# A quarter tile moved from the dense to the gathered half of an expert layer, with new pacing of the background work

## The chip, the cores and the metric
One core of one Trainium2 chip runs the whole kernel. The time is device microseconds of one execution. A profiled execution lists the busy time of each engine: PE is TensorE (PEld its weight loads), DVE VectorE, ACT ScalarE, POOL GpSimd, SP SyncE, which only issues transfers.

## The reference
One decoder block over 1024 tokens of width 1024, in float32. First a token mixer (a pooling branch and a forgetting attention of 16 heads, gated), then a channel mixer with 128 x 128 single-neuron experts, then a norm:

```python
h2 = modulate(rmsnorm(x, norm2_g), sh2, sc2)
q  = einsum('bsd,dk->bsk', h2, w_query)           # 8 heads x 2 halves x 128
sc = einsum('bshpc,hpnc->bshpn', q, sub_keys)     # 128 scores per half
# top 16 of each half, their 256 sums, top 16 of those: idx (expert), gates = softmax
a  = gelu(einsum('cd,chkd->chk', h2, peer_u[idx])) * gates
x += gt2 * einsum('chk,chkd->cd', a, peer_v[idx])
out = rmsnorm(x, final_g)
```

Each token thus uses 128 of the 16,384 experts (8 heads x 16).

## The kernel before, in words
**Precision.** Each float32 product is made of three TensorE passes over a high and a low part (`mm3`, lines 278 to 281). `split` (231) makes the parts: ScalarE writes the high one, VectorE or GpSimd subtracts for the low one. `load_w` (242) loads 512 KB of raw weights and splits them on the chip.

**Phases.** `PHASES` gives three runs of `phase` (481) over 512, 256 and 256 tokens (called pass or phase 1, 2 and 3 in the text, p = 0, 1, 2 in the code). Each projects and attends, head pair by head pair, then multiplies with `w_out` and then with `w_query` (the loop of line 779, 16 chunks), each chunk followed by scores and the top 16 per half on VectorE (lines 799 to 803). In the first phase `load_s` (259) splits the weights and stores both parts to memory; the later phases load both parts (1 MB per chunk) and split nothing.

**Experts, two ways.** A token tile is 128 tokens. Tiles 1 to 5 (`DT0`, `DT1`; 640 tokens, `ND`) are done densely: all 16,384 experts are computed for them and multiplied with a gate table that is zero where an expert isn't chosen. Tiles 0, 6 and 7 are done by gathering: for each of a token's 128 experts one indirect transfer (`gather`, 898) brings a row of 1024 values per token, 512 KB for 128 tokens, and VectorE takes a dot product (line 915) or adds a scaled row (925): 256 gathers a tile. They are issued on GpSimd's queue and turn in `GBUFS` = 3 buffers, in the dense stage in `GMORE` = 2 more.

**Background.** Three kinds of generators run beside the main work. `choose` (808), one per tile, turns the two lists of 16 into the 16 chosen experts and their gates, nearly all on VectorE. `gates` (941), one per dense tile, builds its part of the gate table in 32 rounds (GpSimd line 971, VectorE 973, TensorE 983, ScalarE 984) and stores it to `Gd`. `experts` (905) does a gathered tile. They are parts of the list `bg["todo"]`, taken in order. `tick(us)` (62) is called by the main work with a nominal duration (24 n x 0.00043 for a projection over n tokens); it adds us x `bg["rate"]` to a credit, and generators are advanced while the credit is positive, each `yield` costing what it states. `RATES` gives the rate in phase 2, from phase 3 on, in the dense stage, and from `w_out` of phase 3. `drain` empties the list at once.

**Dense stage.** `dense_experts` (1000): 16 groups. In the `up` half of a group 8 weight chunks (`ut`) each meet 2 halves of the 640 columns, 24 matmuls of 320 columns a half; GELU on ScalarE, the gate multiply (1026) and the split of the result on VectorE. In the `down` half 8 chunks (`vt`) sum over the group into `acc` (1042). A group's gate table (`Gg`, 2.5 MB, one buffer) is loaded at its first `up` (1012). The results of a half go through six PSUM banks. After the last group `finish_dense` (1048) transposes and norms the five tiles; then `drain` issues whatever is left.

The order on each engine is that of the program's issue, subject to the tile framework's own scheduling; `keep_in_program_order` pins the gathers.

Of the kernel before, what the change touches and what calls it, by code (L numbers as in the profile page):

```python
# [7 lines left out]
F = mybir.dt.float32  # L8
R = mybir.dt.float32r
# [8 lines left out]
D = 1024  # L18
# [8 lines left out]
DT0, DT1 = 1, 6  # L27
ND = (DT1 - DT0) * 128
# [12 lines left out]
RATES = (0.75, 0.6, 0.68, 0.7)  # L41
# [5 lines left out]
def block_kernel(ctx: ExitStack, tc: tile.TileContext, I, out, dbg=None):  # L47
# [173 lines left out]
    def rstd(ss):  # L221
        nc.vector.tensor_add(ss[:, 2:3], ss[:, 0:1], ss[:, 1:2])  # L222
        nc.scalar.activation(ss[:, 3:4], ss[:, 2:3], AF.Sqrt, scale=1.0 / D, bias=epsc)
        nc.vector.reciprocal(ss[:, 3:4], ss[:, 3:4])  # L224
        return ss[:, 3:4]
# [166 lines left out]
    def head2(c):  # L392
# [17 lines left out]
        fhl = c.big.tile([48, n], R, name="fhl", tag="fhl", bufs=1)  # L410
# [70 lines left out]
    def phase(c, nxt):  # L481
# [230 lines left out]
        if p == 2:  # L712
            bg["todo"].insert(0, gates(W["gb"], DT1 - 1))
# [32 lines left out]
        dl = [i for i in range(NQ) if DT0 <= qb0 + i < DT1]  # L746
        gl = [i for i in range(NQ) if i not in dl]
        if dl:
            T = slice(dl[0] * 128, dl[-1] * 128 + 128)
            o = (qb0 + dl[0] - DT0) * 128  # L750
            mv(h2dT[0][:, :, o:o + len(dl) * 128], h2h[:, :, T])
            mv(h2dT[1][:, :, o:o + len(dl) * 128], h2l[:, :, T])
            per = D // n
            for b, v in enumerate(tiles):
                mv(x1dT[:, b * per:(b + 1) * per, o:o + len(dl) * 128], v[:, :, T])
# [22 lines left out]
        tx = [sel.tile([128, PH, 2, 16], U32, name="mxi", tag="mxi", bufs=4) for _ in range(NQ)]  # L778
        for ch in range(16):
# [24 lines left out]
        store_parts()  # L804
        big.release()
        return nc_, [choose(qb0 + i, tv[i], tx[i]) for i in range(NQ)]

    def choose(tt, mv_, mx_):
        yield 0.0
        dense = DT0 <= tt < DT1  # L810
# [11 lines left out]
        yield 3.0  # L822
        ts = sel.tile([128, PH, 16], F, name="ts", tag="ts", bufs=1)
        ti = sel.tile([128, PH, 16], U32, name="ti", tag="ti", bufs=1)
        for h in range(PH):
# [6 lines left out]
            if h % 2:  # L832
                yield 1.8
# [31 lines left out]
        gt = sel.tile([128, PH, 16], F, name="gate", tag="gated" if dense else f"gate{tt}", bufs=1)  # L865
# [7 lines left out]
        if not dense or (dbg and "idx" in dbg):  # L873
            ix = sel.tile([128, 128], I32, name=f"idx{tt}")
# [4 lines left out]
        if dense:  # L879
            tr = W["gb"].tile([128, 3, 128], F, name="pairT", tag="pairT", bufs=DT1 - DT0)  # L880
# [5 lines left out]
        if dbg and "idx" in dbg:  # L886
            nc.sync.dma_start(dbg["idx"][tt * 128:(tt + 1) * 128], ix)
            nc.sync.dma_start(dbg["gate"][tt * 128:(tt + 1) * 128], gate[tt])

    X = {"i": 0, "p": None}  # L890
# [13 lines left out]

    def experts(tt):
        yield 0.0
        row = g_row("row")
        nc.sync.dma_start(row, h2d[tt])
        h2 = X["ps"].tile([128, D], F, name="h2", tag="gx", bufs=1)
        nc.scalar.activation(h2, row, AF.Copy)  # L910
        dots = gp.tile([128, 128], F, name="dots", tag="dots", bufs=1)
        for k in range(128):
            yield GSTEP
            g = gather(I["peer_u"], idx[tt][:, k:k + 1])
            nc.vector.scalar_tensor_tensor(g, g, 1.0, h2, op0=OP.mult, op1=OP.mult, accum_out=dots[:, k:k + 1])  # L915
        nc.scalar.activation(dots, dots, AF.Gelu)
        nc.vector.tensor_mul(dots, dots, gate[tt])
        acc = X["ps"].tile([128, D], F, name="acc", tag="gx", bufs=1)
        for k in range(128):
            yield GSTEP  # L920
            g = gather(I["peer_v"], idx[tt][:, k:k + 1])
# [262 lines left out]
```

## Time and profile before

| | |
|---|---|
| runs shown, us | 3359.74, 3362.7, 3367.93 (median 3362.7) |
| profiled execution, us | 3367.48 (span 3365.7) |
| busy in the span | PE 3132.3, DVE 2427.5, ACT 1267.7, POOL 1754.1 |
| instructions | 56,878 |
| DMA | 1004.60 MB, mean 298 GB/s |
| first and last dense matmul, us from the start | 1493.9, 3317.6 |

Busy time is the time in which an engine had at least one instruction under way; matmuls overlap, so a matmul's own duration (some 310 ns) is longer than the step to the next. PEclk is the granted TensorE clock as a share of 2.4 GHz. DMA share is the mean busy share of the core's 16 DMA engines. In a row of a chain or a wait, what stands after `<-` released the instruction.

### The profile page before, as it was taken

What the parts mean: (1) busy time and instruction counts of PE and PEld (TensorE: products, weight loads), DVE (VectorE), ACT (ScalarE), POOL (GpSimd) and SP (SyncE); (2) the same over time, 40 slices, a digit from 0 to 9 for tenths busy, and PEclk for the clock granted to TensorE, in tenths of its full rate; (3) what the DMA queues carried; (4) which work ended last, traced back from release to release, by engine and by line L of the source; (5) the groups of instructions that cost most, each with busy time, mean ns of one, the idle gap of its engine ahead of it and who ended that gap; (6) DMA issues with size and microseconds to landing.
All of it is one profiled execution on the core that took longest, in us unless ns stands there. A gap on an engine that the chain in (4) does not pass through costs nothing. (4 is left out here: it accounts for less than half of the span.)

```text
span 3365.7 us, 56878 instructions
## 1 busy us (share of the span) xinstructions
PE 3132.3 (93%) x20912; PEld 2992.4 (89%) x20912; DVE 2427.5 (72%) x5520; ACT 1267.7 (38%) x2405; POOL 1754.1 (52%) x1328
## 2 busy tenths in 40 slices
PE   6999889888799899888999999999999999999995
PEld 4778778778788798888999999999999999999994
DVE  5764556997958876768766777677677767777677
ACT  5555542346545565522222322232223222322231
POOL 1233233013324132414777787678777767777774
PEclk9999999899999999999999999999999999999997
DMA  8987787777789788783899899899998999989997
GB/s 330 332 299 261 271 297 270 240 231 235 226 304 313 226 268 269 259 311 139 306 333 332 320 328 337 318 348 332 339 329 321 322 330 344 346 319 337 329 337 252
DMA packets 373078, 1004.60 MB, mean 298 GB/s; under 512 B 34128, under 2 KB 146368, under 8 KB 370624
## 3 DMA queue, kind: packets, MB, share of 16 engines
q1 hardware_dynamic: 262208, 598.26, 51.7%
q0 software_dynamic: 110592, 402.70, 32.7%
q8 instruction: 166, 2.72, 0.3%
q14 instruction: 112, 0.92, 0.1%
HBM read 851.25 MB, written 149.58 MB: 297 GB/s over the span
## 5 line engine op out<-in xcount | busy, mean ns | idle before, releaser
L233 POOL TENSOR_TENSOR wl<-wr,wh 128x1024 fp32r<-128x1024 f32 x320 | 776.1, 2426 | 647.7 <-ACT wh L232 604.4
L232 ACT ACTIVATE wh<-wr 128x1024 fp32r<-128x1024 f32 x325 | 344.2, 1059 | 927.5 <-PE oT L280 536.1
L279 PE MATMUL oT<-ah,wh 128*128 128x320 f32 x2048 | 632.3, 310 | 10.0 <-ACT ah L232 10.0
L279 PE MATMUL z<-h2x,wh 128*128 128x320 f32 x2048 | 633.8, 310 | 3.3 <-ACT wh L232 1.7
L281 PE MATMUL z<-h2x,wl 128*128 128x320 f32 x2048 | 633.5, 310 | 1.4 <-POOL wl L233 1.3
L280 PE MATMUL oT<-al,wh 128*128 128x320 f32 x2048 | 633.0, 310 | 1.2 <-DVE al L233 1.1
L280 PE MATMUL z<-h2x,wh 128*128 128x320 f32 x2048 | 633.3, 309 | 0.0
L281 PE MATMUL oT<-ah,wl 128*128 128x320 f32 x2048 | 632.7, 310 | 0.0
L925 DVE SCALAR_TENSOR_TENSOR acc<-g,dots,acc 128x1024 f32<-128x1024 f32 x381 | 489.2, 1284 | 124.9 <-DMA g<-peer_v,idx 122.3
L915 DVE SCALAR_TENSOR_TENSOR g<-g,h 128x1024 f32<-128x1024 f32 x384 | 460.9, 1214 | 94.2 <-DMA g<-peer_u,idx 92.4
L900 POOL DMA_INDIRECT g<-peer_v,idx x384 | 362.0, 943 | 126.1 <-issue 45.7
L900 POOL DMA_INDIRECT g<-peer_u,idx x384 | 361.7, 942 | 124.1 <-issue 57.1
L279 PEld LDWEIGHTS oT<-ah,wh 128*128 128x128 f32 x2048 | 384.9, 188 | 10.5 <-ACT ah L232 10.5
L279 PEld LDWEIGHTS z<-h2x,wh 128*128 128x128 f32 x2048 | 385.0, 188 | 4.2 <-ACT wh L232 2.2
L281 PEld LDWEIGHTS z<-h2x,wl 128*128 128x128 f32 x2048 | 384.8, 188 | 2.4 <-POOL wl L233 2.4
L280 PEld LDWEIGHTS oT<-al,wh 128*128 128x128 f32 x2048 | 385.1, 188 | 1.8 <-DVE al L233 1.8
L281 PEld LDWEIGHTS oT<-ah,wl 128*128 128x128 f32 x2048 | 385.1, 188 | 0.0
L280 PEld LDWEIGHTS z<-h2x,wh 128*128 128x128 f32 x2048 | 384.9, 188 | 0.0
L971 POOL TENSOR_TENSOR o<-hi,lo 128x512 f32<-128x512 f32 x160 | 206.6, 1293 | 322.2 <-PE G L983 283.0
L279 PE MATMUL z<-hTh,wh 128*128 128x256 f32 (+1 forms) x840 | 290.0, 350 | 18.2 <-ACT hTh L232 8.4
L281 PE MATMUL z<-hTh,wl 128*128 128x256 f32 (+1 forms) x840 | 286.3, 341 | 1.0 <-DMA wl<-w_inl 0.8
L280 PE MATMUL z<-hTl,wh 128*128 128x256 f32 (+1 forms) x840 | 285.9, 340 | 1.3 <-DVE hTl L233 1.3
(286 smaller groups left out, 5938.0 us busy)
## 6 DMA issues: line engine op xcount, KB each, us to landing
wr<-ut SPq DMA_DIRECT2D x128, 512.0 KB
wr<-vt SPq DMA_DIRECT2D x128, 512.0 KB
Gd<-Gb SPq DMA_DIRECT2D x40, 1024.0 KB
Gg<-Gd SPq DMA_DIRECT2D x16, 2560.0 KB
wh<-w_inh SPq DMA_DIRECT2D x60, 512.0 KB
wl<-w_inl SPq DMA_DIRECT2D x60, 512.0 KB
wm<-w_mod SPq DMA_DIRECT2D x48, 512.0 KB
wr<-w_in SPq DMA_DIRECT2D x45, 512.0 KB
```

What stands on the lines that cost most here:

```text
L232: nc.scalar.activation(hi, src, AF.Copy)
L233: eng_lo.tensor_tensor(lo, src, hi.bitcast(F), op=OP.subtract)
L279: nc.tensor.matmul(ps, ah, bh, start=start, stop=False)
L280: nc.tensor.matmul(ps, ah, bl, start=False, stop=False)
L281: nc.tensor.matmul(ps, al, bh, start=False, stop=stop)
L900: d = nc.gpsimd.indirect_dma_start(out=g, out_offset=None, in_=table, in_offset=bass.IndirectOffsetOnAxis(ap=col, axis=0))
L915: nc.vector.scalar_tensor_tensor(g, g, 1.0, h2, op0=OP.mult, op1=OP.mult, accum_out=dots[:, k:k + 1])
L925: nc.vector.scalar_tensor_tensor(acc, g, dots[:, k:k + 1], acc, op0=OP.mult, op1=OP.add)
L971: nc.gpsimd.tensor_tensor(o2, hi[:, X, :, None].to_broadcast([128, 4, 8, 16]), lo[:, X, None, :].to_broadcast([128, 4, 8, 16]), op=OP.mult)
```

## The change
1. The dense part covers tokens 32 to 639 (`DA`, `DB`, 608 columns, halves of 304) instead of tiles 1 to 5. Gathered are tiles 5, 6, 7 and the first `HK` = 32 tokens of tile 0. These 32 x 128 rows are laid out as 128 partitions x 32: four blocks of 32 experts, each with a copy of the 32 tokens; so 32 gathers for `u`, 32 for `v`, and the four partial sums are added at the end.
2. This quarter tile runs as background in phase 3; if it isn't finished then, it goes on in the dense stage. Outside the dense stage its rows use SBUF (`x_tile`) and the three buffers.
3. `w_query` is loaded raw and split in every phase; nothing of it is stored.
4. The costs that `choose` states are half as high again, `RATES` are new, and the rate is 0 in the `w_query` loop. `choose` of tile 5 moves to the dense stage; there each `choose` stands right before its own `experts`.
5. A group's gate table is loaded in four parts, at the second, fourth, sixth and eighth `down` of the group before. The dense stage has one more pair of weight buffers.

```diff
-RATES = (0.75, 0.6, 0.68, 0.7)
+RATES = (0.95, 1.0, 0.8, 1.0)
...
+        if name == "w_query":
+            return load_w(I[name][i])
...
-            bg["todo"].insert(0, gates(W["gb"], DT1 - 1))
             bg["rate"] = RATES[3]
...
+        rate, bg["rate"] = bg["rate"], 0.0
         for ch in range(16):
...
         store_parts()
+        bg["rate"] = rate
...
-        yield 3.0
+        yield 4.5
...
-                yield 1.8
+                yield 2.7
...
-                        yield 0.8
+                        yield 1.2
...
-                yield 1.1
+                yield 1.6
...
     def experts(tt):
         yield 0.0
+        n, K = (HK, HK) if tt == HT else (128, 128)
         row = g_row("row")
-        nc.sync.dma_start(row, h2d[tt])
+        ix, gt = idx[tt], gate[tt]
+        if tt == HT:
+            ix = sel.tile([128, HK], I32, name="ixh", tag="ixh", bufs=1)
+            gt = sel.tile([128, HK], F, name="gth", tag="gth", bufs=1)
+            for b in range(128 // HK):
+                to, c = slice(b * HK, b * HK + HK), slice(b * HK, b * HK + HK)
+                nc.sync.dma_start(ix[to], idx[tt][:HK, c])
+                nc.sync.dma_start(gt[to], gate[tt][:HK, c])
+                nc.sync.dma_start(row[to], h2d[tt][:HK])
+        else:
+            nc.sync.dma_start(row, h2d[tt])
...
-        for k in range(128):
+        for k in range(K):
             yield GSTEP
...
+        if tt == HT:
+            for b in range(1, 128 // HK):
+                nc.sync.dma_start(r1[:n], r0[b * n:b * n + n])
+                nc.vector.tensor_tensor(r0[:n], r0[:n], r1[:n], op=OP.add)
+                r1 = g_row("r1")
...
-        for q in range(32):
+        for q in range(DA // 4 if tt == HT else 0, 32):
...
-        W["x"], W["m"], W["i"] = dd, 1, 2
+        W["x"], W["m"], W["i"] = dd, 2, 3
...
+        def load_gates(gr, part):
+            if part == 0:
+                A["G"] = dd.tile([128, NC16, 8, 16], F, name="Gg", tag="Gg", bufs=1)
+            C = slice(part * NC16 // 4, (part + 1) * NC16 // 4)
+            nc.sync.dma_start(A["G"][:, C], Gd[gr][:, C].rearrange("p c (i t) -> p c i t", i=8))
...
             wh, wl = load_w(I["vt"][gr * 8 + c], nc.gpsimd)
+            if gr < 15 and c % 2:
+                load_gates(gr + 1, c // 2)
...
-    late = [experts(tt) for tt in range(DT0)]
-    bg["todo"] = ch[:DT0] + [f for i in range(DT0, 4) for f in (ch[i], gates(gb, i))]
+    early = [experts(HT)]
+    bg["todo"] = [f for i in range(4) for f in (ch[i], gates(gb, i))]
     bg["rate"] = RATES[0]
     c, ch = phase(c, next_head(2))
     W["xq"].release()
-    bg["todo"] += [f for i in range(4, DT1) for f in (ch[i - 4], gates(gb, i))][:-1]
+    bg["todo"] += [ch[0], gates(gb, 4)] + early
+    late = ch[1:]
     bg["rate"] = RATES[1]
     c, ch = phase(c, lambda: None)
+    early = [f for f in bg["todo"] if f in early]
+    bg["todo"] = [f for f in bg["todo"] if f not in early]
     drain()
...
-    bg["todo"] = ch + late + [experts(tt) for tt in range(DT1, 8)]
+    bg["todo"] = early + [f for i, tt in enumerate(range(DT1, 8)) for f in ((late + ch)[i], experts(tt))]
     bg["rate"] = RATES[2]
     dense_experts()
```

## Rows read from the trace of the kernel before

**Rows 1.** Busy time by stretch: from and to in us, length, busy us of each engine with its instructions, then the granted clock, the DMA share and GB/s. The stretches: phase 2 up to its query loop, that loop, phase 3 in two halves up to `w_out`, its query loop, the start of the dense stage, its steady part, all of it.

```profile
605.00:980.00 375.00, 316.48 (x2358) 302.59 (x2359) 313.06 (x969) 203.71 (x449) 94.94 (x84) 0.91 0.75 244
980.00:1055.00 75.00, 71.83 (x588) 70.38 (x587) 56.29 (x274) 26.07 (x48) 24.33 (x23) 0.98 0.92 318
1055.00:1230.00 175.00, 155.90 (x1187) 144.86 (x1187) 155.14 (x481) 101.00 (x223) 50.03 (x51) 0.96 0.80 252
1230.00:1403.00 173.00, 159.89 (x1274) 152.86 (x1273) 117.67 (x237) 103.46 (x209) 57.53 (x50) 0.97 0.82 262
1425.00:1491.00 66.00, 57.02 (x431) 54.76 (x431) 35.95 (x214) 16.98 (x35) 7.25 (x4) 0.92 0.97 344
1493.90:1600.00 106.10, 91.55 (x577) 88.62 (x578) 96.04 (x329) 32.61 (x53) 43.45 (x24) 0.92 0.43 155
1600.00:3300.00 1700.00, 1700.00 (x11593) 1700.00 (x11593) 1219.76 (x1860) 456.56 (x737) 1278.95 (x981) 1.00 0.91 330
1493.90:3318.00 1824.10, 1809.55 (x12291) 1806.61 (x12292) 1332.53 (x2207) 489.17 (x790) 1331.28 (x1012) 1.00 0.88 319
```

**Rows 2.** Matmuls in order of time: start in us, duration, then line and shape. First and last of 51 in a row at 320 columns in the dense stage, of 18 at 256 in a query loop, of 20 at 512 in the first query loop.

```profile
1639.72 0.31 PE L280 MATMUL z<-h2x,wh 128*128 128x320 f32 x1
...
1647.06 0.31 PE L279 MATMUL z<-h2x,wh 128*128 128x320 f32 x1
...
1485.03 0.28 PE L279 MATMUL z<-h2h,wr 128*128 128x256 f32 x1
...
1487.03 0.28 PE L281 MATMUL z<-h2h,wr 128*128 128x256 f32 x1
...
551.62 0.39 PE L280 MATMUL z<-h2l,wh 128*128 128x512 f32 x1
...
555.97 0.39 PE L281 MATMUL z<-h2h,wl 128*128 128x512 f32 x1
```

**Rows 3.** The end, in order of time: the last dense matmul, the last norm of a dense tile, the last gather on GpSimd, the last operation of the last gathered tile.

```profile
3317.59 0.31 PE L281 MATMUL oT<-ah,wl 128*128 128x320 f32 x1
...
3344.49 1.40 DVE L1060 SCALAR_TENSOR_TENSOR Gg<-z,ss,h2x 128x512 f32<-128x512 f32 x2
...
3349.55 0.94 POOL L900 DMA_INDIRECT g<-peer_v,idx  x1 [3.76 <-DVE acc L925]
...
3360.77 1.28 DVE L938 SCALAR_TENSOR_TENSOR r<-r,ss,r 128x1024 f32<-128x1024 f32 x1
```

**Rows 4.** Groups of instructions by line and shape, background work: count, then busy us, mean ns of one, idle time before. Eight `choose` and five `gates` in all; lines 827 to 831 are a head's five steps, two of which are shown.

```profile
L858 DVE SCALAR_TENSOR_TENSOR cand<-pk 128x128 f32<-128x128 f32 x256 | 82.1, 457 | 0.1
L862 DVE TENSOR_REDUCE pk<-cand 128x128 f32<-128x1024 f32 x32 | 38.7, 1209 | 0.2
L828 DVE FIND_INDEX8 ti<-ts,cand 128x8 uint32<-128x96 f32 x64 | 15.2, 248 | 0.0
L829 DVE MATCH_REPLACE8 tmp<-ts,cand 128x96 f32<-128x96 f32 x64 | 15.0, 237 | 0.1
L973 DVE TENSOR_TENSOR o<-iota,pairT 128x512 f32<-128x512 f32 x160 | 133.6, 839 | 33.1 <-PE G L983 32.2
L958 DVE TENSOR_TENSOR lo<-iota,dg 128x256 f32<-128x256 f32 x40 | 17.3, 438 | 0.0
L958 DVE TENSOR_TENSOR hi<-iota,dg 128x128 f32<-128x128 f32 x40 | 11.8, 304 | 7.4 <-POOL o L971 7.4
```

**Rows 5.** The same view: the weight splits, and VectorE's own work in the dense stage.

```profile
L233 POOL TENSOR_TENSOR wl<-wr,wh 128x1024 fp32r<-128x1024 f32 x320 | 776.1, 2426 | 647.7 <-ACT wh L232 604.4 <-DMA kdh<-ks 10.3 <-PE pt L628 8.8
L232 ACT ACTIVATE wh<-wr 128x1024 fp32r<-128x1024 f32 x325 | 344.2, 1059 | 927.5 <-PE oT L280 536.1 <-PE z L280 191.7 <-DMA wr<-vt 134.3
L1026 DVE TENSOR_TENSOR z<-z,Gg 128x320 f32<-128x320 f32 x256 | 126.6, 495 | 66.2 <-ACT z L1024 64.4
L233 DVE TENSOR_TENSOR al<-z,ah 128x320 fp32r<-128x320 f32 x256 | 124.0, 485 | 22.7 <-ACT ah L232 22.6
L1042 DVE TENSOR_TENSOR accT<-accT,oT 128x320 f32<-128x320 f32 x240 | 116.0, 484 | 182.2 <-PE oT L281 182.0
```

**Rows 6.** The gathers' DMA queue over the span (packets, MB, share of 16 engines), and two stretches of 10 us in the dense stage (columns as in rows 1).

```profile
q0 software_dynamic: 110592, 402.70, 32.7%
...
2820.00:2830.00 10.00, 10.00 (x70) 10.00 (x69) 4.40 (x11) 0.00 (x0) 6.17 (x5) 1.00 1.00 419
...
2400.00:2410.00 10.00, 10.00 (x70) 10.00 (x69) 6.60 (x13) 1.38 (x2) 7.98 (x8) 1.00 0.96 326
```

**Rows 7.** VectorE's work per gather, by line and shape as in rows 4, and the time of a gather from issue to landing.

```profile
L925 DVE SCALAR_TENSOR_TENSOR acc<-g,dots,acc 128x1024 f32<-128x1024 f32 x381 | 489.2, 1284 | 124.9 <-DMA g<-peer_v,idx 122.3
L915 DVE SCALAR_TENSOR_TENSOR g<-g,h 128x1024 f32<-128x1024 f32 x384 | 460.9, 1214 | 94.2 <-DMA g<-peer_u,idx 92.4 <-DVE accT L1042 0.3
...
L915 DVE DVE_READ_ACCUMULATOR g<-g,h 128x1 f32 x384 | 31.7, 83 | 0.0
...
DMA to landing us min/median/max: 4.2/6.0/14.9
```

**Rows 8.** VectorE's rounds of the gate table (line 973) in the two halves of phase 3, and the index search of `choose` (line 858, 32 for one) in the first: length, busy us and count.

```profile
1055.00:1230.00 175.00, 25.79 (x33) 0.96 0.80 252
1230.00:1403.00 173.00, 32.02 (x39) 0.97 0.82 262
...
1055.00:1230.00 175.00, 19.18 (x64) 0.96 0.80 252
```

More of the change, by code (lines that the diff above doesn't have):

```diff
@@ L745, in phase @@
         z0, = to_T(c, x1, rsb, sc2, sh2, h2h, h2l, [("w_query", 0)])
[L746 to L752, printed above, removed]
+        lo, hi = max(t0, DA), min(t0 + n, DB)
+        gl = [i for i in range(NQ) if not DA <= t0 + i * 128 <= DB - 128]
+        if lo < hi:
+            T = slice(lo - t0, hi - t0)
+            O = slice(lo - DA, hi - DA)
+            mv(h2dT[0][:, :, O], h2h[:, :, T])
+            mv(h2dT[1][:, :, O], h2l[:, :, T])
             per = D // n
             for b, v in enumerate(tiles):
-                mv(x1dT[:, b * per:(b + 1) * per, o:o + len(dl) * 128], v[:, :, T])
+                mv(x1dT[:, b * per:(b + 1) * per, O], v[:, :, T])
         if gl:
@@ L809, in choose @@
         yield 0.0
-        dense = DT0 <= tt < DT1
+        dense = tt < DT1
+        gathered = tt == HT or not dense
         buf = sel.tile([128, 1024], F, name="cand", tag="cand", bufs=1)
@@ L860, in choose @@
                     if x % 4 == 3:
-                        yield 0.8
+                        yield 1.2
                 nc.vector.tensor_reduce(to, oh.rearrange("p h k x -> p (h k) x"), axis=AX.X, op=OP.add)
-                yield 1.1
+                yield 1.6
             nc.vector.tensor_add(dst, dst, pf)
-        gt = sel.tile([128, PH, 16], F, name="gate", tag="gated" if dense else f"gate{tt}", bufs=1)
+        gt = sel.tile([128, PH, 16], F, name="gate", tag="gate" if gathered else "gated", bufs=3 if gathered else 1)
         nc.vector.tensor_tensor(gt, ts, ts[:, :, 0:1].to_broadcast([128, PH, 16]), op=OP.subtract)
@@ L872, in choose @@
         gf = gt.rearrange("p h k -> p (h k)")
-        if not dense or (dbg and "idx" in dbg):
-            ix = sel.tile([128, 128], I32, name=f"idx{tt}")
+        if gathered:
+            ix = sel.tile([128, 128], I32, name=f"idx{tt}", tag="idx", bufs=3)
             nc.vector.scalar_tensor_tensor(ix, w0, 128.0, w1, op0=OP.mult, op1=OP.add)
@@ L885, in choose @@
             pairT[tt] = tr
[L886 to L890, printed above, removed]
+    X = {"i": 0, "p": None, "ps": None}
     def g_row(name):
@@ L1054, in finish_dense @@
                 for c in range(4):
-                    nc.tensor.transpose(pt[:, c * 128:(c + 1) * 128],
-                                        acc[:, hf * 4 + c, i * 128:(i + 1) * 128], ident)
-                nc.scalar.activation(yt[:, H], pt, AF.Square, accum_out=ss[:, hf:hf + 1])
-            rs = rstd(ss)
+                    nc.tensor.transpose(pt[:n, c * 128:(c + 1) * 128], acc[:, hf * 4 + c, T], ident)
+                nc.scalar.activation(yt[:n, H], pt[:n], AF.Square, accum_out=ss[:n, hf:hf + 1])
+            rs = rstd(ss, n)
             for pt, H in zip(ps, hs):
-                nc.vector.scalar_tensor_tensor(yt[:, H], pt, rs, fg[:, H], op0=OP.mult, op1=OP.mult)
-            nc.sync.dma_start(out[(DT0 + i) * 128:(DT0 + i + 1) * 128, :], yt)
+                nc.vector.scalar_tensor_tensor(yt[:n, H], pt[:n], rs, fg[:n, H], op0=OP.mult, op1=OP.mult)
+            nc.sync.dma_start(out[DA + T.start:DA + T.stop, :], yt[:n])
+        for part in range(4):
+            load_gates(0, part)
         for gr in range(16):
@@ L1074, in dense_experts @@
                 down(gr, i)
-        for i in range(DT1 - DT0):
-            finish_dense(i, rows, fg[:, 0])
+        for i in range((ND + 127) // 128):
+            finish_dense(i, rows[:, i * D:i * D + D] if i < 4 else fg[:, 1], fg[:, 0])
         W["m"], X["p"] = 0, None
```

61 lines of the change are left out of this document (34 added, 27 removed).

## The prediction
> **What bounds the kernel now.** Read first the table of stretches [rows 1], by stage. In the dense stage (1493.9 to 3318, 54% of the span) TensorE is busy in all 1700 us between 1600 and 3300, at granted clock 1.00, while the DMA engines are 0.91 busy at 330 GB/s and VectorE is at 72%: the stage is TensorE's own time, with little left on the transfers. The list of matmuls in order of time gives the step from one to the next: 7.34 us over 50 steps at 320 columns = 146.8 ns, 2.00 us over 17 at 256 columns = 117.6 ns, 4.35 us over 19 at 512 = 229 ns [rows 2], so the step goes with the columns (0.456 ns each between 256 and 320) and weights loaded for every matmul don't set it. 12,288 x 0.1468 = 1804 us of the stage's 1824. In the second and third attention phases (605 to 1491) no engine is full: VectorE is at 83%, 75%, 89%, 68% and 54% of the five stretches, TensorE at 84 to 96%, DMA at 0.75 to 0.97. There the order of work and the loads decide together. Last, the chain of waits: the span ends 48 us after the last dense matmul, on gathers still to be issued [rows 3].
>
> **Dense stage, columns.** 640 columns become 608, halves of 320 become 304; the count of matmuls stays. One step falls by 16 x 0.456 = 7.3 ns to 139.5; 12,288 x 7.3 ns = 90 us off, 1714 us left. Ends: 6.9 ns (the slope between 320 and 512, 0.428 ns) gives 84, and 0 if something else sets the pace (below).
> The row for 320 columns is 146.8 ns. The Trainium skill, TensorE: Matmul & The Clock Gate, section Back-to-back issue gap, gives a warm step of N/2.4 + 2.5 ns, 135.8 ns here; the trace does not agree in height or slope, and by it the saving would be 6.7 ns x 12,288 = 82 us instead of 90.
>
> **Dense stage, start.** From 1493.9 to 1600 TensorE loses 14.5 us and runs at mean clock 0.92: two `choose` runs stand first, 0.92 of VectorE is spent and no gather moves (DMA 0.43) [rows 1]. One `choose` costs VectorE about 34 us: 32 x 0.46 + 4 x 1.21 for the index search, 8 heads x 1.45 for the top 16, the rest small [rows 4]. Afterwards one stands there, at 34.3 planner units over rate 0.8 instead of two of 24 over 0.68. One planner unit of the stage lasts 1.066 us (24 matmuls are counted as 3.137 and take 24 x 0.1393 = 3.343). So 34 us of VectorE in 46 us beside the stage's own 21% (per group of 768 matmuls 16 x 0.47 + 16 x 0.46 + 16 x 0.46 = 22 of 107 us, [rows 5] times 0.95): 95%, it fits. I take 18 of the 20 us beyond 1804 as saved. Ends 0 and 20.
>
> **Dense stage, gathers.** 768 gathers of 524 kB remain (tiles 5, 6, 7 for 0, 6, 7). Each is paced at 1.46 units: before 1.46/0.68 x 1.066 = 2.29 us, after 1.46/0.8 x 1.066 = 1.94 us. Demand while they run, before: 0.524 MB/2.29 us = 229 GB/s, weights 0.524 per 48 matmuls (7.05 us) 74, gate table 2.62 MB per 768 matmuls 23: 327, as measured (330). After: 270 + 78 + 23 = 371 GB/s. The measured rate at full share is 330/0.91 = 363 [rows 1]; q0's own figures give 402.7 MB/(0.327 x 3365.7) = 366 [rows 6]. 371 is above either. The gathers' stretches last 1125.7 units /0.8 x 1.066 = 1499 us at TensorE's pace; at 363 GB/s they last 1499 x 371/363 = 1532. With gather DMAs late, VectorE, in order, holds the gate multiply behind them, PSUM fills and TensorE waits. I add 35 us, rounded. Ends: 0 (windows of 10 us reached 419 GB/s), and 206 if the ceiling is the 326 GB/s of a window with share 0.96 [rows 6]; 363 is the mean over the whole stage, so I take it. VectorE then needs 768 x 1.29 + 370 + 102 = 1463 us [rows 5, 7], 84%; GpSimd 2.43 per 48 matmuls and 0.94 per gather, also 85%: neither binds first.
> Full share and 419 GB/s stand in the row of a 10 us window [rows 6]. The Trainium skill, DMA: Bandwidth & Descriptors, section Where 436 GB/s comes from, lets the memory side bind at about 358 GB/s per core; the trace does not agree for a core alone, and with 358 the loss would be 54 us instead of 35.
> The gate table in four parts, issued while the group before is in its `down` half, takes SyncE's wait for the last gate multiply away from ahead of the `ut` loads; TensorE shows no wait in 1600 to 3300, so it is worth 0, and the same holds for the fourth pair of weight buffers. SyncE may wait at part 0 for the last multiply, with `vt` loads queued behind; the weight buffers cover that wait.
>
> **End.** The plan: 3 x (34.3 + 375.2) = 1228.7 units of background against a credit of 256 x 24 x 608 x 0.00043 x 0.8 = 1285, so gathers end about 56/0.8 x 1.066 = 75 us before the last matmul. Before it was 1174 against 1150, and some 16 were left. What follows the last matmul is then five transposes-and-norms of about 2 us each, a first one of 5 us and 4 us of writing: 20 us for 48. 28 us off; ends 0 and 32.
>
> **Query weights.** Pass 2 (980 to 1055) and pass 3 (1425 to 1491) read 16 x 1.05 MB, and 5.2 MB of `h2x` in pass 3: 23 MB in 66 us at share 0.97. After, 0.52 MB each: 14.4 MB, 42 us at that rate. What is late next: TensorE, 57 us busy in pass 3; the splits (ACT 1.06, GpSimd 2.43 per chunk, 17 and 39 us for 16, [rows 5]) hide under it, on a GpSimd 7 of 66 us busy. Background is at rate 0 there. I take 56 us for each: 19 and 10 off; ends 0 and 25 together with 33. In pass 1 the 16.8 MB of stores go: 2 us at most.
>
> **Phases, background.** Units in the code: phase 2 has 209.6 ticks outside the query loop x 0.95 = 199 credited; its list is 256.8 (4 x 34.3 + 23.9 + 3 x 31.9), so 57.7 goes over. Phase 3 adds 34.3 + 31.9 + 94.9 = 218.8 in all, against 205.1 + 21.1 = 226 at rate 1.0: the quarter tile just fits. In phase 2 outside the query loop VectorE's background is 3.25 x 34 + 2.75 x 33 = 201 us against 3.9 x 34 + 2 x 33 = 199: the same, evener. I take 8 off. Ends -15 and +15.
> Phase 3 (1055 to 1403, 348 us): VectorE does 272.8 us, of it two `choose` and 72 gate rounds of 0.839 + (0.438 + 0.304)/4 = 1.02 us [rows 1, 4, 8], own work 131. After: 131 + 1.75 x 34 + 64 x 1.02 + 64 x 1.29 for the quarter tile's gathers = 339 us, 97% of the old stretch. And DMA: 33.5 MB for 64 gathers = 92 us of full share, less 2 MB of gates, where 0.81 of 348 us = 282 is already spent: 369. So it cannot stay at 348. At phase 2's VectorE share (313/375 = 0.835) 339 us need 406; at full share of the DMA, 369. I take 401: +53. Ends +21 (the DMA sum) and the 3-buffer limit of rival 2. The copies of the quarter tile's rows and sums wait on SyncE for VectorE with weights queued behind, a few us inside this sum.
>
> **Sum.** -90 - 18 + 35 - 28 - 29 - 2 - 8 + 53 = -87 on the profiled execution's 3367.5 us (span 3365.7), 3280; the median of the runs, 3362.7, is 4.8 lower: 3276.
>
> **Rivals.** (1) The transfers' ceiling binds in the dense stage, ends slower: at 340 GB/s the gather stretches take 1499 x 371/340 = 1636, 137 instead of 35: 3378; it decides against the change from a loss of 122 us, a ceiling of 343. For it: 10 us windows with share 0.96 at 326. Against: 363 as the mean, 419 as best. (2) In phase 3 only three gather buffers turn: landing 6.0 us (4.2 to 14.9) + 1.3 + 0.4 over three is 2.6 us each [rows 7], 165 us for 64; at 14.9 it is 354 us, 189 more: 3465. It cancels the gain from a landing of 10 us. Against: the median. (3) Neither binds (phase 3 absorbs the quarter tile, DMA carries 371): 3276 - 35 - 53 = 3188; for it the 419 GB/s window and TensorE's 9% of unused time in phase 3. (4) The quarter tile isn't done by phase 3: up to 1323.6 units against 1285 leaves 26 gathers at the end, 60 us, but phase 3 is 38 shorter: 3298.
>
> **Chances.** Forecast 0.51 (3235 to 3325), (1) 0.13, (2) 0.09, (3) 0.23, (4) 0.04. Slower: 0.09 of (1) and 0.05 of (2); same: 0.04 and 0.03; the rest faster. 0.3% is 10 us, about what such a measurement can tell from none. The range reaches to both sides, 3200 to 3380.
>
> **What would show it.** Right: steps of 139 ns at 304 columns, small TensorE waits on gathers in the dense stage with DMA share over 0.95, no gather after the last matmul, the third phase some 50 us longer, both later query loops near 56 us. Wrong: TensorE below 90% in the dense stage, or a third phase over 480 us.

## The result and the profile after

The changed kernel takes 3412.4 us (median of 4 runs, 3401.7 to 3420.4) against 3362.4 for the kernel before: ratio 1.0145 (95% interval 1.0109 to 1.018), slower by about 50 us, where 3276 was predicted. Its profiled execution took 3418.5 us with a span of 3416.8. The traces of b_comb and b_inter72, two of the experiments below, were taken in slow executions and are not read; the medians are of fast ones.

The parts of the page of the changed kernel on busy time and on the DMA queues, and the shares by engine of the chain that ended last:

```profile
PE 3060.0 (90%) x20856; PEld 2914.0 (85%) x20856; DVE 2566.5 (75%) x5616; ACT 1291.5 (38%) x2445; POOL 1888.6 (55%) x1415
...
q1 hardware_dynamic: 257328, 563.56, 48.2%
q0 software_dynamic: 119808, 436.26, 35.0%
...
PE 49%; DVE 8%; DMA 5%; issue 2%; POOL 1%; ACT 1%; SPq 0%; POOLq 0%; DVEq 0%; ACTq 0%
```

TensorE has 72 us less to do than before (3132.3 then), VectorE 139 us more. Then the windows, with the columns of [rows 1]: phase 2, its query loop, phase 3 in two halves, its query loop, the start of the dense stage, the rest of it, and what follows the last dense matmul.

```profile
605.00:980.00 375.00, 322.66 (x2457) 308.36 (x2457) 312.12 (x873) 212.99 (x460) 117.66 (x106) 0.94 0.77 247
984.60:1059.00 74.40, 68.86 (x518) 66.77 (x518) 42.20 (x237) 34.97 (x55) 49.31 (x24) 0.91 0.61 190
1055.00:1230.00 175.00, 147.31 (x1069) 136.44 (x1069) 155.02 (x479) 91.26 (x199) 47.43 (x48) 0.92 0.70 225
1230.00:1400.00 170.00, 156.42 (x1231) 148.39 (x1230) 116.61 (x243) 102.53 (x216) 55.43 (x51) 0.97 0.87 282
1445.50:1535.00 89.50, 66.50 (x440) 62.99 (x441) 83.92 (x278) 32.04 (x59) 63.78 (x38) 0.85 0.86 297
1535.50:1788.00 252.50, 218.41 (x1468) 214.78 (x1468) 247.08 (x584) 71.60 (x115) 146.72 (x99) 0.94 0.69 240
1788.00:3294.00 1506.00, 1506.00 (x10825) 1506.00 (x10824) 1102.33 (x1706) 417.60 (x685) 1160.66 (x884) 1.00 0.92 335
3312.00:3398.00 86.00, 0.00 (x0) 0.00 (x0) 73.76 (x62) 0.29 (x1) 51.62 (x56) 0.50 0.96 353
```

Three things are to be seen against [rows 1]. In the seventh row TensorE is full, as before, and 1506 us over 10,825 matmuls make 139.1 ns each: the saving by columns came. In the last row it does nothing for 86 us, while VectorE does 62 instructions behind gathers at DMA share 0.96. In the fifth the query loop of phase 3 takes 89.5 us (74.7 before). Cut at the first and the last dense matmul, the spans give:

| us | before | after | difference | predicted |
|---|---|---|---|---|
| start of the dense stage | 1493.9 | 1535.5 | +41.6 | +14 |
| dense stage | 1823.7 | 1758.8 | −64.9 | −73 |
| after the last dense matmul | 48.1 | 122.5 | +74.4 | −28 |

So the dense stage came out near its prediction in sum (by terms that cancel, as is told below), and the loss stands on both sides of it.

The gathers tell why. First, the rows of the full tiles' and the quarter tile's gathers on GpSimd in the changed kernel (duration, first and last start); then GpSimd's gathers alone, busy us and count, in the same 1200 us of the kernel before and, in the third fence, of the changed one:

```profile
L905 POOL DMA_INDIRECT g<-peer_u,idx x384: 932/938/1685, 1622.1 to 3158.1; - x192
L905 POOL DMA_INDIRECT g<-peer_v,idx x384: 932/937/1228, 1983.6 to 3398.8; - x192
L905 POOL DMA_INDIRECT g<-peer_u,ixh x32: 932/950/1784, 1374.1 to 1503.8; - x32
L905 POOL DMA_INDIRECT g<-peer_v,ixh x32: 932/951/2002, 1508.0 to 1654.1; - x32
```

```profile
2000.00:3200.00 1200.00, 491.56 (x523) 1.00 0.91 332
```

```profile
2000.00:3200.00 1200.00, 492.61 (x523) 1.00 0.92 336
```

523 gathers in 1200 us in either kernel, one every 2.29 us. The shorter matmuls and the planner's faster rate changed nothing about that pace. From the first to the last of the 768 it is 1766 us before (1583.2 to 3349.5) and 1777 after (1622.1 to 3398.8). The first one is 39 us later and the whole 11 us longer: together that is 49 of the 51 us by which the span grew.

### The profile page after: what moved, and what is told of

Same layout as the page of the kernel before. It is cut to its first block, busy times and chain, and to the rows that moved or that the text cites. A ratio compares the mean times of both kernels' runs of the same rounds, so it can differ in the third digit from the quotient of the medians.

```text
span 3416.8 us, 56946 instructions
## 1 busy us (share of the span) xinstructions
PE 3060.0 (90%) x20856; PEld 2914.0 (85%) x20856; DVE 2566.5 (75%) x5616; ACT 1291.5 (38%) x2445; POOL 1888.6 (55%) x1415
## 4 chain that ended last, share of the span: by engine, by line
PE 49%; DVE 8%; DMA 5%; issue 2%; POOL 1%; ACT 1%; SPq 0%; POOLq 0%; DVEq 0%; ACTq 0%
PE z L287 8%; PE z L286 8%; PE z L285 8%; PE oT L286 8%; PE oT L285 8%; PE oT L287 8%; DMA g<-peer_v,idx 2%; DVE g L938 1%; DVE acc L948 1%; DVE cand L866 1%; POOL g L905 1%; PE G L1013 1%; DMA wl<-w_outl 1%; DMA wh<-w_inh 0%; DMA wr<-w_inl 0%
## 5 line engine op out<-in xcount | busy, mean ns | idle before, releaser
L237 POOL TENSOR_TENSOR wl<-wr,wh 128x1024 fp32r<-128x1024 f32 x352 | 854.3, 2428 | 485.4 <-ACT wh L236 460.2
L236 ACT ACTIVATE wh<-wr 128x1024 fp32r<-128x1024 f32 x357 | 377.8, 1058 | 899.0 <-PE oT L286 247.7
L285 PE MATMUL z<-h2x,wh 128*128 128x304 f32 x2048 | 621.2, 303 | 13.1 <-DVE al L237 7.3
L286 PE MATMUL oT<-al,wh 128*128 128x304 f32 x2048 | 619.5, 303 | 9.8 <-DVE al L237 9.8
L285 PE MATMUL oT<-ah,wh 128*128 128x304 f32 x2048 | 618.2, 303 | 6.4 <-ACT ah L236 3.4
L287 PE MATMUL z<-h2x,wl 128*128 128x304 f32 x2048 | 618.2, 302 | 4.7 <-POOL wl L237 4.7
L286 PE MATMUL z<-h2x,wh 128*128 128x304 f32 x2048 | 620.5, 303 | 0.0
L287 PE MATMUL oT<-ah,wl 128*128 128x304 f32 x2048 | 615.4, 301 | 0.0
L938 DVE SCALAR_TENSOR_TENSOR g<-g,h 128x1024 f32<-128x1024 f32 x416 | 515.3, 1252 | 108.2 <-DMA g<-peer_u,idx 102.2
L948 DVE SCALAR_TENSOR_TENSOR acc<-g,dots,acc 128x1024 f32<-128x1024 f32 x412 | 544.9, 1323 | 55.6 <-DMA g<-peer_v,idx 47.9
L285 PEld LDWEIGHTS oT<-ah,wh 128*128 128x128 f32 x2048 | 386.5, 189 | 7.5 <-ACT ah L236 4.3
L1001 POOL TENSOR_TENSOR o<-hi,lo 128x512 f32<-128x512 f32 x152 | 192.0, 1266 | 255.3 <-PE G L1013 214.1
```

Of the source, the lines that this page charges most:

```text
L236: nc.scalar.activation(hi, src, AF.Copy)
L237: eng_lo.tensor_tensor(lo, src, hi.bitcast(F), op=OP.subtract)
L285: nc.tensor.matmul(ps, ah, bh, start=start, stop=False)
L286: nc.tensor.matmul(ps, ah, bl, start=False, stop=False)
L287: nc.tensor.matmul(ps, al, bh, start=False, stop=stop)
L948: nc.vector.scalar_tensor_tensor(acc, g, dots[:, k:k + 1], acc, op0=OP.mult, op1=OP.add)
```

## The experiments

Each row below is cut as above; "gathers" are the 768 of the full tiles, from the first start to the last. A name with a_ is an edit of the changed kernel, with b_ of the kernel before. b_comb and b_inter72 have no cut. a_gmore4_1gate and the kernels with a_noht and a_ht in their names leave out or falsify a part of the output; they show what a part costs and are no way out.

| kernel | median, us | ratio to before (95% interval) | dense stage | gathers | after last dense matmul |
|---|---|---|---|---|---|
| before | 3362.4 | | 1493.9 to 3317.6 | 1583 to 3350 | 48.1 |
| after | 3412.4 | 1.0145 (1.0109 to 1.018) | 1535.5 to 3294.3 | 1622 to 3399 | 122.5 |
| a_gmore4 | 3414.3 | 1.0144 (1.012 to 1.0169) | 1539.0 to 3393.4 | 1622 to 3314 | 19.9 |
| a_m1 | 3413.5 | 1.0154 (1.0121 to 1.0186) | 1528.2 to 3286.8 | 1613 to 3392 | 123.3 |
| a_gmore4_1gate | 3370.8 | 1.0018 (1.0007 to 1.0029) | 1537.7 to 3357.6 | 1622 to 3279 | 19.7 |
| a_rate68 | 3507.5 | 1.0436 (1.0408 to 1.0464) | 1526.7 to 3286.0 | 1612 to 3486 | 218.3 |
| a_noht | 3320.6 | 0.9871 (0.9849 to 0.9892) | 1500.8 to 3238.6 | 1551 to 3300 | 79.0 |
| a_htg8 | 3364.7 | 1.0 (0.9985 to 1.0015) | 1544.2 to 3283.1 | 1594 to 3344 | 78.9 |
| a_htdve | 3397.5 | 1.0105 (1.0078 to 1.0133) | 1531.8 to 3281.7 | 1594 to 3379 | 113.8 |
| a_noht_wqold | 3305.7 | 0.9825 (0.9795 to 0.9854) | 1497.4 to 3235.3 | 1539 to 3291 | 73.4 |
| a_wqold | 3408.3 | 1.0127 (1.0109 to 1.0145) | 1518.3 to 3281.0 | 1625 to 3397 | 134.9 |
| b_inter | 3370.4 | 1.0023 (1.001 to 1.0035) | 1486.5 to 3316.1 | 1489 to 3349 | 50.8 |
| b_comb | 3355.5 | 0.9965 (0.9951 to 0.998) | | | |
| b_inter72 | 3342.3 | 0.9928 (0.9913 to 0.9943) | | | |
| b_rate72 | 3336.6 | 0.9911 (0.9896 to 0.9927) | 1493.8 to 3316.2 | 1574 to 3304 | 19.1 |

### Two more gather buffers, and the fourth pair of weights

```diff
-GMORE = 2
+GMORE = 4
-        W["x"], W["m"], W["i"] = dd, 2, 3
+        W["x"], W["m"], W["i"] = dd, 1, 2
```

> The changed kernel with four instead of two extra gather buffers in the dense stage (seven in all), and one pair of extra weight buffers instead of two to make room. Theory (five buffers limit the gathers in the order that the framework writes out, 47 a group where the planner asks for 55): the built order has 55 a group, so no gather is left behind the last dense norm; the 122 us after the last dense matmul fall to about 20, the start stays as it is, and the time is about 3412 - 100 = 3312 us (3295 to 3335). Rival (the transfers' ceiling): the same bytes have to move at 335 GB/s, the dense stage grows by what the tail loses, 3390 to 3415 us.

a_m1 has the second half of the edit alone:

> The changed kernel with one pair of extra weight buffers in the dense stage instead of two, five gather buffers as in the changed kernel: the kernel with seven gather buffers had both edits. Theory (gathers in flight crowd out the weight loads, not the missing pair): dense stage 1759 and 122 us after it as in the changed kernel, 3405 to 3420. Rival (the missing pair made TensorE wait there): dense stage 1800 or more, 3440 and above.

a_m1 measures what the changed kernel does (1.0154), so the missing pair is not what a_gmore4 shows. a_gmore4 has no gathers left at the end, and yet no gain: its dense stage is 96 us longer than after's. Its window while gathers run, then its gathers alone in the same 1200 us as above:

```profile
1789.00:3333.00 1544.00, 1487.52 (x10439) 1473.67 (x10439) 1159.95 (x1745) 407.87 (x677) 1205.22 (x944) 0.98 0.95 347
...
2000.00:3200.00 1200.00, 534.43 (x568) 0.98 0.96 348
```

568 gathers instead of 523, one every 2.11 us. Against a_m1 only the number of buffers differs, so it had set the pace of 2.29 us; how it did is told under "The written order". But TensorE is no longer full (1487.5 of 1544 us, clock 0.98). The waits say on what, first in the changed kernel, then in a_gmore4, both from 1790 to 3333 us (total, times, longest in us; in the kernel before the first of them is 126.1, 16, 12.2):

```profile
ACT wh L236 <- DMA wr<-vt: 209.9, 36, 16.0
...
DVE g L938 <- DMA g<-peer_u,idx: 101.4, 80, 4.4
```

```profile
ACT wh L236 <- DMA wr<-vt: 462.8, 76, 17.1
...
PE oT L287 <- POOL wl L237: 39.3, 21, 5.0
...
PE oT L285 <- ACT wh L236: 11.7, 10, 1.9
```

With five buffers VectorE waits for gathers. With seven, the weights come late: ScalarE waits more than twice as long for `vt`, and TensorE for both halves of the split. Dense stage and what follows it sum to 1871.8 us before, 1881.3 after, 1874.3 in a_gmore4.

Next, in a_gmore4, 15 of the 16 gate tables (37 MB) are not loaded, to take transfers away:

```diff
-            if gr < 15 and c % 2:
+            if False:
```

> The kernel with seven gather buffers, with the gate table loaded once instead of 16 times (15 tables of 2.49 MB are left out; all groups use that of the first). Theory (transfers bind in the dense stage once the gathers are placed in it): 37 MB less at some 340 to 350 GB/s is 107 to 110 us of transfers, more than the 91 us that TensorE loses after 1789 us, so the stage falls from 1854 to 1765 to 1800 us and the time from 3414 to 3325 to 3360. Rival (VectorE's or GpSimd's order, or the latency of a gather, holds the stage): the time stays within 15 us of 3414.

The time, 3370.8 us, lies between the two ranges. The dense stage fell by 34 us, less than the 54 expected at least. Transfers are part of the price, but TensorE still isn't full:

```profile
1789.00:3358.90 1569.90, 1530.21 (x10821) 1515.44 (x10821) 1193.74 (x1801) 420.23 (x693) 1214.88 (x937) 0.99 0.90 320
...
2000.00:3200.00 1200.00, 1169.55 (x8272) 1157.47 (x8271) 909.25 (x1358) 324.75 (x538) 956.77 (x745) 1.00 0.92 331
```

At share 0.92 it starts 8272 matmuls in these 1200 us, where the changed kernel at share 0.92 and 336 GB/s starts 8623 and is full. So the rate of the transfers alone doesn't decide it. What the rest is stays open.

### The planner's rate

```diff
-RATES = (0.95, 1.0, 0.8, 1.0)
+RATES = (0.95, 1.0, 0.68, 1.0)
```

> The changed kernel with the dense stage's rate put back from 0.8 to 0.68. Theory (buffers cap the built order): the order keeps 47 gathers a group and about 17 more are left to the end: 3412 + 17 x 2.0 = 3445 us at most, 3415 at least, so 0.8 had bought little. Rival (transfers' ceiling): the dense stage loses its gather waits and gets shorter by what the tail gains, within 10 us of 3412.

It cost 95 us, more than either expectation. A group of the dense stage still uses up 47 gathers, and after the last dense matmul 87 are issued, against 66 in the changed kernel. These 21 are near the 17 expected, but each gather behind the stage takes longer. GpSimd's gathers alone there, first in a_rate68, then in the changed kernel:

```profile
3310.00:3480.00 170.00, 69.54 (x75) 0.50 0.77 236
```

```profile
3312.00:3398.00 86.00, 51.62 (x56) 0.50 0.96 353
```

One comes every 2.27 us in the first, every 1.54 in the second. 1606.2 units x 0.68 are 1092 of credit against 1228.7 units: 137 short, so 93 gathers are left to the last `drain`, and there `X["p"]` is `None` and only three buffers turn. At 0.8 the credit suffices and every gather is issued with five. So 0.8 for 0.68 did not hurry the gathers of the dense stage; it kept the last ones out of the three buffers.

### The written order

The framework writes each engine's order down beforehand, with a timeline of its own. Both kernels without that:

```diff
-schedule_with_timeline_sim=True
+schedule_with_timeline_sim=False
```

> The changed kernel without the framework's reordering by a simulated timeline: each engine's order is that in which the program issues. Theory (the order, not the chip, put the gathers late): quarter tile done before the dense stage, 55 gathers a group, nothing after the last norm; the tail falls from 122 to about 20 us; with five buffers the gathers of 1.94 us each make VectorE wait in the dense stage, at most 60 us. Without the reordering the phases may lose some, as the before kernel without it will show: 3290 to 3370. Rival (transfers' ceiling): the dense stage grows by 80 us or more, 3400 or above.

> The kernel before, without the framework's reordering. Its built order in the dense stage is already that of the issue (49 gathers a group either way), so both theories expect no change there; what differs from 3362 is what the reordering is worth in the phases. Expected 3362 to 3400.

a_nosim takes 3690.4 us (1.097, 1.0948 to 1.0992) and b_nosim 3630.3 (1.0793, 1.0768 to 1.0817): the reordering is worth 278 and 268 us, and a_nosim's theory and b_nosim's range are missed by more than 200. Without it a_nosim has nothing left at the end (20.4 us), but a dense stage of 1934. That is in the rival's range, yet it doesn't speak for the transfers: from 2000 to 3200 us their share is 0.86 (314 GB/s), and b_nosim, whose groups have 49 gathers as before, has a stage of 1941.

The written order itself explains the end of the changed kernel. VectorE's last sums over gathered rows, in order of time:

```profile
3315.39 1.40 DVE L1096 SCALAR_TENSOR_TENSOR h2x<-z,ss,h2x 96x512 f32<-96x512 f32 x2
3316.71 1.28 DVE L948 SCALAR_TENSOR_TENSOR acc<-g,dots,acc 128x1024 f32<-128x1024 f32 x1
...
3406.10 1.29 DVE L948 SCALAR_TENSOR_TENSOR acc<-g,dots,acc 128x1024 f32<-128x1024 f32 x1 [0.78 <-DMA g<-peer_v,idx]
3407.42 1.22 DVE L952 TENSOR_TENSOR r<-acc,r 128x1024 f32<-128x1024 f32 x1
```

59 of these sums (L948) stand behind the last dense norm (L1096). Counted in the trace, most dense groups of 768 matmuls use up 47 or 48 gathers, where the planner's rate meant 55. In the kernel before they use up 49 to 51, where the planner meant 49; in b_rate72 50 or 51, where it meant 52; in a_gmore4 mostly 55 or 56, and none is left. As long as TensorE is full, this count is the pace: 47 gathers in 768 x 139.1 ns are one every 2.27 us. It is not the time that five buffers need to come round, for behind the dense stage the same five give one every 1.54 us (above). More buffers let the framework put more gathers into a group; why five make it stop at 47 is not shown. On the chip the chain of waits runs through the 59, from 3293 to 3407 us:

```profile
3325.44 5.38 DMA g<-peer_v,idx
3330.91 1.30 DVE acc L948
...
3338.68 6.17 DMA g<-peer_v,idx
...
3406.10 1.30 DVE acc L948
3407.42 1.24 DVE r L952
...
3411.64 1.28 DVE r L968
```

A line "DMA g" here is a gather's way to the buffer, which the next sum waits for; from 3325 on it comes back every 8 to 14 us, after some five to nine gathers at 1.5 us each.

The order also undid a part of the change. The four parts of a gate table were to be spread over four `down`; in most groups all four stand together on SyncE's queue, ahead of `vt` loads. The lists of SyncE, ScalarE and GpSimd in one group of the changed kernel:

```profile
2602.89 2.00 SPq L1044 DMA_DIRECT2D Gg<-Gd  x4
2605.47 20.28 SPq L248 DMA_DIRECT2D wr<-vt  x3
...
2621.86 1.06 ACT L236 ACTIVATE wh<-wr 128x1024 fp32r<-128x1024 f32 x1 [13.29 <-DMA wr<-vt]
...
2623.00 2.40 POOL L237 TENSOR_TENSOR wl<-wr,wh 128x1024 fp32r<-128x1024 f32 x1 [8.94 <-ACT wh L236]
```

ScalarE waits 13.3 us for `vt`, GpSimd 8.9 us for ScalarE, and the gathers behind this split on GpSimd's queue stop with it. TensorE stays full, so no matmul is lost by that. Whether the order would hold more gathers with the table loaded as before was not tried.

### The quarter tile

It is left out in a_noht, reduced to one gather in 8 in a_htg8, and to an eighth of VectorE's columns in a_htdve:

```diff
-    early = [experts(HT)]
+    early = []
...
+            if tt != HT or k % 8 == 0:
...
+            N = slice(0, 128) if tt == HT else slice(0, D)
```

> The changed kernel without the quarter tile's gathers (the first 32 tokens of the output are left out). Theory (the quarter tile costs the phases and the dense start): query loop of phase 3 back to about 60 us from 110, dense stage starts at 1470 to 1490 instead of 1535, and what is left after the last dense matmul falls, since no leftover gathers stand ahead: 3300 to 3350. Rival (the phases lose it to the new pace of `choose` and `gates`, not to the gathers): the dense stage starts at 1520 or later, 3390 to 3412.

> The changed kernel with one gather for every eight of the quarter tile's 64 (each row is used eight times; its output is wrong), VectorE's work as it was. Theory (gathers through three buffers): the quarter tile is done before the dense stage, which starts at 1500 to 1515; 3330 to 3355. Rival (VectorE's time): 3390 to 3412.

> The changed kernel with the quarter tile's VectorE work cut to 128 of 1024 values per row (its 32 tokens of output are wrong); its 64 gathers stay. Without the quarter tile the kernel took 3321, with it 3412: 92 us. Theory (its gathers are slow through three buffers beside the phase's own loads, and that puts it late): 3385 to 3412. Rival (its 83 us of VectorE time are the cost): 3325 to 3350.

The quarter tile costs 92 us (3412.4 − 3320.6); of that the full number of gathers accounts for 48, VectorE's arithmetic at full width for 15, and neither is the whole: a_htg8 misses its range, a_htdve is in that of the theory. On the spans of the two profiled executions (99 us apart), 34.7 us stand before the dense stage, 21.0 in it, 43.5 behind it. The 34.7 us before the stage come back only where the whole quarter tile is gone: the stage starts at 1544.2 in a_htg8 and at 1531.8 in a_htdve, against 1535.5 and 1500.8 (a_noht). So the number of gathers isn't what delays the start; what they cost lies in the stage and behind it. The rows of the eight gathers in a_htg8:

```profile
L905 POOL DMA_INDIRECT g<-peer_u,ixh x4: 938/1002/1134, 1375.5 to 1406.4; - x4
L905 POOL DMA_INDIRECT g<-peer_v,ixh x4: 936/1542/2831, 1411.4 to 1439.8; - x4
```

They start before the query loop, the last at 1440; the 32 of each in the changed kernel run from 1374 to 1654, 4.4 us apart in the mean, through the whole query loop and 119 us into the dense stage. The first gather of a full tile stands at 1622 us, against 1551 in a_noht. In a_noht the loop of phase 3 has:

```profile
1429.90:1500.70 70.80, 58.97 (x444) 56.46 (x445) 39.84 (x233) 29.91 (x57) 39.59 (x17) 0.94 0.61 200
```

70.8 us instead of 89.5 (the 110 of the expectation is not what the trace shows), with VectorE at 40 us for 84.

### The query weights

```diff
-        if name == "w_query":
-            return load_w(I[name][i])
```

a_noht_wqold takes these two lines out of a_noht, a_wqold out of the changed kernel; b_comb has them in the kernel before, and b_inter72 is b_comb without them.

> The kernel without the quarter tile, and with the query weights stored and loaded in two parts as before. The query loops lasted 71 and 75 us before and 75 and 71 in the kernel without the quarter tile, so raw weights brought nothing in them: expected the first query loop 8 us longer, the other two the same, 3320 to 3335. Rival (raw weights are worth the 29 us of the prediction, hidden by something else): 3340 to 3355.

> The changed kernel with the query weights stored again as in the kernel before, everything else as changed. Theory (splitting them anew costs, as a_noht_wqold against a_noht showed with 15 us): 3390 to 3402 us, second query loop back near 71 us and the dense stage starting some 10 us earlier. Rival (that gain belongs to the kernel without the quarter tile; here the third query loop waits for the quarter tile's gathers and needs the free transfers): 3405 us or above.

> b_comb without the query weights split anew: the kernel before, with choose and gathered tiles taken in turn and the pace of the third phase's planner at 0.72 for 0.68. Theory (splitting anew costs about 15 us in any of these kernels): 3335 to 3347 us, against 3355.5 for b_comb. Rival (it costs nothing here, b_comb's small gain is the pace's): 3350 to 3360 us.

Split anew, the weights cost 15 us in a_noht (3320.6 − 3305.7), 13 in the kernel before (3355.5 − 3342.3) and 4 in the changed kernel, which is within the spread of its runs. So the expectation for a_noht_wqold was missed by more than 14 us on the good side, that for a_wqold was the rival's, and that for b_inter72 came. (Its edit, `RATES[2]`, is the rate of the dense stage, not of the third phase.) In a_wqold the stage's start does get 17 us earlier, but the gathers don't (1625 against 1622), and they end the kernel. In the second query loop the DMA share fell from 0.91 to 0.61 and the time did not: TensorE is busy 68.9 us of 74.4, and before was 67.9 of 71.1:

```profile
978.70:1049.80 71.10, 67.90 (x550) 66.45 (x551) 53.33 (x265) 24.73 (x46) 21.56 (x20) 0.98 0.91 315
```

In the third loop of the changed kernel TensorE also waits for the new splits and, once, for `h2h` (waits of 1445.5 to 1535 us: total, times, longest):

```profile
PE z L287 <- POOL wl L237: 13.3, 9, 3.0
...
PE z L285 <- ACT h2h L236: 11.8, 1, 11.8
...
PE z L285 <- ACT wh L236: 8.3, 3, 7.3
```

### Pace and order in the kernel before

```diff
-    bg["todo"] = ch + late + [experts(tt) for tt in range(DT1, 8)]
+    bg["todo"] = late + [f for x, tt in zip(ch, range(DT1, 8)) for f in (x, experts(tt))]
...
-RATES = (0.75, 0.6, 0.68, 0.7)
+RATES = (0.75, 0.6, 0.72, 0.7)
```

The first is b_inter, the second b_rate72, both are in b_inter72, and with the query weights split anew in b_comb.

> The kernel before with one edit: in the dense stage the gathered tile 0 comes first and each of the two `choose` stands right before its tile, instead of both at the start. If the loss at the start of the dense stage (14.5 us of TensorE, clock 0.92, no gather under way for 90 us) is these two, the stage gets 10 to 20 us shorter and fewer gathers are left at the end: 3330 to 3350. If it is the first loads of the stage, 3355 to 3365.

> The kernel before with that edit, raw query weights split in every phase, and the dense rate 0.72 for 0.68 so that no gather is left at the end. Gathers then need 0.524 MB per 2.16 us = 243 GB/s, with weights and gates 341 in all, below the 350 at which the seven-buffer kernel saturates. Theory: 20 us from the query loops, 15 from the start, 25 from the end: 3290 to 3320. Rival (the raw weights bring nothing, or the transfers bind at 341): 3335 or above.

> The kernel before with only the pace changed, 0.68 to 0.72: 43 units (1.46 each, 29 gathers) more are let in during the dense stage, where some 16 were left. Theory (transfers have 9% left at this demand, so a little more goes in): tail 48 to about 22, dense stage longer by 0 to 12, 3337 to 3352 us. Rival (the transfers are the sum, dense and tail together stay at 1872): 3358 to 3368 us.

b_inter starts its gathers 94 us earlier and ends them at the same time, so it gains nothing (3370.4 us, above both ranges); with 0.72 in b_inter72 it takes 28 us less, so the rate held the last ones back. b_comb is a miss by 35 us and more. b_rate72, one number in the kernel before, is the fastest version with a whole output: 3336.6 us, 0.9911. (Of the 43 units of its expectation 24 are let in, the 16 gathers that were left; the rest is to spare.) Its window before the last dense matmul and the one behind it:

```profile
1743.80:3316.20 1572.40, 1572.40 (x10723) 1572.40 (x10722) 1153.10 (x1705) 426.42 (x685) 1185.14 (x913) 1.00 0.92 333
3316.20:3335.30 19.10, 6.95 (x43) 5.31 (x41) 10.51 (x24) 8.99 (x29) 0.00 (x0) 0.67 0.42 166
```

TensorE is full to the end, no gather follows (GpSimd 0.00), and the dense stage is as long as before (1822.4). The reordered list on top of that, b_inter72, is no better.

## Why the prediction was wrong

**Dense stage, columns: right.** 139.1 ns a step against 139.5. That the whole stage took 1758.8 us against 1751 (1824 − 90 − 18 + 35) is luck: the 18 us at its start were not saved and the 35 us of late gathers did not come.

**End: this step failed.** "gathers end about 56/0.8 x 1.066 = 75 us before the last matmul" rested on the planner's credit. A step earlier each gather was "paced at 1.46 units", 1.94 us after. In the kernel before, the planner's 2.29 us and the measured 2.29 us are the same number, and the trace could not tell whether the planner or the written order with five buffers made it; I took the planner. Three runs say the order and the buffers: after keeps 2.29 at a planned 1.94, b_rate72 has 2.28 at a planned 2.16, and two more buffers bring 2.11 (568, above). In b_rate72 GpSimd's gathers alone, in the same 1200 us:

```profile
2000.00:3200.00 1200.00, 495.67 (x527) 1.00 0.93 335
```

The written order shows where the remainder went: behind the last norm, where 66 gathers were still to be issued at the last dense matmul, not none. With five buffers and a rate of 0.72 or 0.8 the 768 gathers take 1730 to 1784 us from first to last in each kernel of the table, whatever the matmuls take. So the shorter dense stage was given back at the end: 20 us were predicted for it and 122 came.

**Dense stage, gathers.** The 35 us did not come (TensorE is full from 1788 to 3294), because the demand of 371 GB/s did not come. Where it is let in, in a_gmore4, 347 GB/s is the mean at share 0.95, and the stage grows by 96 us, nearer to the 137 of rival 1 than to 35. The ceiling of 363, a mean rate divided by its share, was reached in no stage here, and a_gmore4_1gate shows that the 96 us are not the transfers' alone. The Trainium skill, DMA: Bandwidth & Descriptors, section Where 436 GB/s comes from, gives about 358 GB/s per core for the memory side; the tail's 353 GB/s at share 0.96 lies nearer to it than the prediction granted, and a_gmore4's 347 below both. That "the weight buffers cover that wait" holds for TensorE, which stays full, but not for ScalarE and GpSimd (13.3 and 8.9 us in the group above).

**Dense stage, start.** 18 us were to be saved; the changed kernel loses 34 of the first 252 instead (218.4 us busy), with VectorE at 0.98. The sum "95%, it fits" left out the quarter tile, whose gathers and sums lie there to 1654. But the step fails without it too. The first 250 us of the stage in the kernel before, in a_noht and in b_inter:

```profile
1493.90:1743.90 250.00, 235.45 (x1558) 232.52 (x1559) 193.54 (x510) 67.11 (x106) 151.21 (x106) 0.97 0.70 251
```

```profile
1500.80:1750.80 250.00, 233.32 (x1617) 230.47 (x1616) 242.58 (x635) 70.50 (x113) 159.14 (x116) 0.97 0.76 267
```

```profile
1486.50:1736.50 250.00, 234.07 (x1518) 231.04 (x1519) 223.36 (x553) 65.50 (x105) 171.79 (x129) 0.96 0.84 298
```

TensorE loses 14.6, 16.7 and 15.9 us: with one `choose` ahead, or none, as much as with two. So fewer `choose` at the front did not give the time back; what takes it there stays open. (VectorE's share there was 96.0 of 106.1 us, 0.905; the 0.92 is the clock of that row.)

**Phases.** Phase 3 outside its loop grew by 20 us (366.6 to 386.5), under the +21 that was the low end, but because the quarter tile's work moved on into the loop. "Background is at rate 0 there" was true of the planner: the gathers had been issued, and the order on the engines put them there. Each took 4.4 us, against 2.6 in rival 2, between that rival's median and its worst; but its mechanism, three buffers in turn, is not shown. Of the 280 us from the first to the last, GpSimd stands idle 70 ahead of these gathers until VectorE has freed a buffer, and no run changed the number of buffers there. Phase 2 grew by 14 us, within the range of −15 and +15; a_noht has 9 of it.

**Query loops.** −29 were predicted, +18 came (+3 and +15). The step "14.4 MB, 42 us at that rate" took transfers for the bound because their share was 0.97; the windows of [rows 1] also missed the loops, which last 71.1 and 74.7 us, not 75 and 66. TensorE's 57 of 66 us and 68 of 71 us left 3 to 9 us to gain at most, and GpSimd's split now stands on its path. Taking the edit back gave 13 and 15 us in two kernels. In the first loop, where 2 us at most were to go with the stores, 7 went (117.0 to 110.4 us; b_rate72, without the edit, has 112.6).

Rival 1 holds in part, as the price of the way out, and rival 4 in part: 59 sums were left, not by the planner's credit but by the written order. No rival had the written order of the dense stage as the bound.

What stays open: what limits a_gmore4_1gate beside the transfers; where the 13 us go when the query weights are split anew in the kernel before, since b_comb has no cut; what delays the start of the stage in a_htg8 and a_htdve; and whether the quarter tile would pay with more buffers in phase 3, which was not tried. The new costs of `choose`, the new rates of the phases, the rate of 0 in the query loop and the gate table in four parts were not taken back one by one.

## What to carry to other kernels

When a stage's end is set by a second chain (here the gathers), measure that chain's own length from its first to its last instruction before shortening the main work: in the kernel before it ended 32 us after the stage that was to be shortened, so a shorter stage alone could bring nothing. A planner's rate is a wish; the number of buffers and the order finally written decide, and where two paces agree in one trace, only a run that changes one tells which one binds. Count in the trace how many pieces of the second chain the written order puts beside each piece of the main work. The query loop with its transfers at 0.91 and TensorE at 0.95 gained nothing from fewer bytes.

## What was not expected

The reordering by the framework is worth 8% in the kernel before (3630.3 against 3362.4 us). The transfers carry 335 GB/s at share 0.92 with TensorE full for 1500 us, and at 348 GB/s and share 0.96 it starts 6% fewer matmuls (8124 for 8623 in the same 1200 us); the rate isn't all of it, since a_gmore4_1gate starts 8272 at 331 GB/s. And 0.04 in one planner rate made the kernel before 0.9% faster, while its dense stage stayed within 2 us.
